# From the trunk to the up tiles: the chunks in the order first, third, second, and the up operand sums spread over the second chunk's up tiles

## The chip, the cores and the metric

The kernel runs on one core of a Trainium2 chip. The metric is the device time of one execution in microseconds (us), the median of several runs. The profile is one execution taken by the hardware profiler. Its engines: PE (TensorE, matmuls; PEld is its weight load), DVE (VectorE), ACT (ScalarE), POOL (GpSimd), and SP, which issues most DMAs. Each engine works through its own queue in order; between engines, and between DMAs and engines, semaphores order the work.

## The reference

One layer of a streaming encoder, for 1024 prompt frames and 32 sample frames of width D = 1024, 1056 columns in all:

```
h = rms_norm(x, g_mix);  z = h @ w_in -> q, k, v, conv_h, conv_B, conv_C, gate_a, gate_b
a  = window_attention(q, k, v) @ w_attn_out
bo = (conv_B * causal_conv3(conv_C * conv_h)) @ w_conv_out
x += (sigmoid(gate_a) * a + sigmoid(gate_b) * bo) @ w_mix_out
x += cross_attention(rms_norm(x, g_cross) @ w_cq, mem_k, mem_v) @ w_co     # 4 heads, 256 memory rows
x += square(relu(rms_norm(x, g_mlp) @ w_up)) @ w_down                      # hidden 4096
y  = rms_norm(x, g_final)
```

All arithmetic is float32. The sample frames have their own memory keys and values. The change touches the stages from w_conv_out to w_up.

## The kernel before

Activations lie with features on the partitions, eight blocks f of 128 features, and the 1056 columns in three chunks: chunk 0 and chunk 1 with 384 columns, chunk 2 with 288 (256 prompt and the 32 sample columns). Each float32 operand is split into a rounded high half (an ACT copy) and the remainder as low half (a DVE subtraction), and each product is three matmuls: high x high, high x low, low x high. One gemm tile is 8 x 3 = 24 matmuls into one accumulator in PSUM; there are three such accumulators (acc). Weight tiles have two raw buffers (wr) and three buffers each for high and low halves (wh, wl). issue_w splits a weight tile, two tiles ahead of its use. Every second tile of the weights that are used once per chunk is kept: its low half is stored to DRAM on first use (L162) and loaded from there later (L156) in place of the DVE subtraction.

The work is a list of items, filled in program order by item; a scheduler then decides the order within each engine, except that instructions under pin keep their program order. PE's order is fixed in the built program.

For each chunk c the trunk has 16 items: eight do_conv_out (L1030 multiplies the accumulator by the gate) and eight do_mix (L1045 adds the residual; L262 and L263 scale by the gain and split). After the trunk of a chunk come cross_steps(c): chunk_stats (the sum of squares over partitions as small matmuls pq, L214; L216 to L221 compute the inverse root; L229 and L230 put it on a diagonal; two matmuls pr, L231 and L232, spread it over the partitions; L242 copies it to R), two do_cq (queries), the units Cross (one per head, and one for the sample columns in chunk 2) with scores, turn and values, two do_co (four output features each, L1183 to L1185, added to x1 by L1187, squared by L257 and summed by POOL, L259), and chunk_stats again. These steps are laid beside the items of the next stage by beside: after each filler item comes one step. So PE has a full gemm between the short dependent steps.

The order of the chunks is 0, 1, 2. cross_steps(0) lie beside trunk(1), cross_steps(1) beside trunk(2), cross_steps(2) beside the eight up tiles of chunk 0 and the eight of chunk 1 (up0). Then follow the eight up tiles of chunk 2, and then the rest of the up product in late pairs (up_start, up_pair), which form some products by sums of operands.

The up tiles of chunks 0 and 1 take normalised operands: normed_split(c, f) multiplies by gain and R (L1212, DVE), stores the result to DRAM (xn_d), copies the high half (L1215, ACT) and subtracts (L1216, DVE); its DVE operations are pinned. For chunk 2 the operand is only scaled by the gain, and R is applied at the eviction (L1240). Chunk 0's eight normed_split stand after the fillers 6 to 13 of trunk(2), chunk 1's after the fillers 0 to 7 of up0(0) + up0(1).

combine(k), for k = 0 to 3, loads four normalised blocks from xn_d, forms the sums N3, N1, T2 and N4 (three DVE operations, one on POOL) and splits each. Before, it follows the first four up tiles of chunk 2. For k of 2 and 3, T2 and N4 are put into chunk 1's operand buffers (yslot(1)), which are free once chunk 1's up tiles are done.

Of the kernel before, what the change touches and what calls it, by code (L numbers as in the profile page):

```python
# [10 lines left out]
F32 = mybir.dt.float32  # L11
F32R = mybir.dt.float32r
AF = mybir.ActivationFunctionType
ALU = mybir.AluOpType
# [9 lines left out]
NF = 8  # L24
# [14 lines left out]
def hybrid_step(ctx: ExitStack, tc: tile.TileContext, io):  # L39
    nc = tc.nc  # L40
    act, dve, pool_e, pe, sp = nc.scalar, nc.vector, nc.gpsimd, nc.tensor, nc.sync
# [3 lines left out]
    def nm(s):  # L45
        uid[0] += 1
        return f"{s}_{uid[0]}"
# [5 lines left out]
    def closed(cm):  # L53
        cm.__exit__(None, None, None)
# [17 lines left out]
    def col(j):  # L72
        return prm[:, j : j + 1]
# [19 lines left out]
    def pin(ins):  # L93
        return tc.keep_in_program_order(ins)
# [6 lines left out]
    def tmp(n, dt=F32):  # L101
        return tp.tile([P, n], dt, tag="ct", bufs=NCT, name=nm("ct"))
# [11 lines left out]
    def item(fn, *keys):  # L114
        plan.append((fn, keys))
        worder.extend(keys)
# [127 lines left out]
    def chunk_stats(c):  # L244
        chunk_col(c)
        chunk_row(c)
# [508 lines left out]
    def yslot(c):  # L755
        return slot(Y["pool" if c < 2 else "top"], f"Y{c}", CH[c][1])
# [8 lines left out]
    def open_top():  # L765
        Y["cm"], Y["top"] = opened("ytop", bufs=16, reuse_waits="tile", side="right")
# [11 lines left out]
    def pump(n):  # L778
        for into, at, t, get in coming:
            hi, lo = into[at] = (get(), get())  # L780
            pin(act.copy(hi, t))  # L781
            pin(dve.tensor_sub(lo, t, hi.bitcast(F32)))  # L782
        coming.clear()
        for into, at, src, cols, get in wanted[:n]:
            t = cols() if callable(cols) else tmp(cols)
            sp.dma_start(t, src)
            coming.append((into, at, t, get))
        del wanted[:n]
# [76 lines left out]
    def close_gates():  # L865
        pump(0)
        assert not wanted
        closed(Y["cm"])
        open_top()
        ctx.push(Y["cm"])  # L870
        for c in (1, 2):
            wanted.extend((bcp[c], k, bc_d[c][:, k], CH[c][1], lambda c=c: yslot(c)) for k in range(NF))
        pump(2)

# [139 lines left out]
    def mslot(n):  # L1014
        return mpool.tile([P, 384], F32R, tag="M", name=nm("M"))[:, :n]
# [67 lines left out]
    def do_cq(c, j):  # L1083
        def fn(w):
            n = CH[c][1]
            a = acc_tile([P, n])
            gemm(a, w, xc[c])
            t = tmp(n)
            dve.scalar_tensor_tensor(t, a, 0.125, R[c], op0=ALU.mult, op1=ALU.mult)  # L1089
            for e in range(2):  # L1090
                own, other = slice(64 * e, 64 * e + 64), slice(64 - 64 * e, 128 - 64 * e)
                q = yslot(c)
                act.copy(q[own], t[own])
                dve.tensor_sub(q[other], t[own], q[own].bitcast(F32))
                qc[2 * j + e, c] = q

        return fn
# [109 lines left out]
    def lt(n=384):  # L1207
        return L["pool"].tile([P, n], F32, tag="lt", bufs=6, name=nm("lt"))

    def normed_split(c, f):  # L1210
        t = tmp(CH[c][1])
        pin(dve.scalar_tensor_tensor(t, x1[c][f], col(G_MLP + f), R[c], op0=ALU.mult, op1=ALU.mult))  # L1212
        sp.dma_start(xn_d[c][:, f], t)
        hi, lo = xm[c][f] = (yslot(c), yslot(c))
        act.copy(hi, t)  # L1215
        pin(dve.tensor_sub(lo, t, hi.bitcast(F32)))  # L1216
# [16 lines left out]
    def up_part(w, c, j):  # L1233
        n = CH[c][1]
        a = ps.tile([P, n], F32, tag="pt", bufs=2, name=nm("pa")) if w[0] == "late" else acc_tile([P, n])
        gemm(a, w[-2:], xm[c])
        flush()
        t = tmp(n)
        if c == 2:
            dve.scalar_tensor_tensor(t, a, 0.0, R[c], op0=ALU.max, op1=ALU.mult)  # L1240
        else:
            dve.tensor_scalar_max(t, a, 0.0)  # L1242
        h = tmp(n)
        pool_e.tensor_tensor(h, t, t, op=ALU.mult)  # L1244
        hidden(c, j, h)

    def do_up(j, c):
        return (lambda w: up_part(w, c, j)), ("w_up", j)


    comb = {}

    def comb_slot(kind, k):
        if kind in ("N1", "N3"):
            return mslot(384)
        return L["pool"].tile([P, 384], F32R, tag="hx", bufs=8, name=nm("hx")) if k < 2 else yslot(1)

    def combine(k):
        b12, b22, b11, b21 = (lt() for _ in range(4))
        for t, c, f in ((b12, 1, k), (b22, 1, k + 4), (b11, 0, k), (b21, 0, k + 4)):  # L1260
            sp.dma_start(t, xn_d[c][:, f])
        n3, n1, t2, n4 = b22, b12, b11, b21
        pin(dve.tensor_sub(n3, b12, b22))
        pin(dve.tensor_sub(n1, b11, b12))
        pin(dve.tensor_sub(t2, b11, n3))
        pin(pool_e.tensor_tensor(n4, b21, t2, op=ALU.subtract))
        for kind, x in (("T2", t2), ("N1", n1), ("N3", n3), ("N4", n4)):
            hi, lo = comb[kind, k] = (comb_slot(kind, k), comb_slot(kind, k))
            act.copy(hi, x)
            if kind[0] == "T" or kind == "N1":  # L1270
                pin(dve.tensor_sub(lo, x, hi.bitcast(F32)))
            else:
                pin(pool_e.tensor_tensor(lo, x, hi.bitcast(F32), op=ALU.subtract))

# [30 lines left out]
    def up_fetch(i):  # L1307
        if i < len(UP):
            pair_fetch(("u", i), io["w_up"][UP[i][0]], io["w_up"][UP[i][1]])

    def up_issue(i, which):
        if i < len(UP):
            pair_issue(("u", i), which)
        elif which != 2:
            if worder[wpos[0]] is STOP:
                wpos[0] += 1
            issue_w()
# [129 lines left out]
    def cross_steps(c):  # L1447
        units = [Cross(c, h) for h in ([0, 1, 2, 3] if c < 2 else [4, 0, 1, 2, 3])]
        nu = len(units)
        steps = [("call", [mem_load] if c == 0 else [mem_load_s] if c == 1 else [])]  # L1450
        steps.append(("call", [lambda: chunk_stats(c)]))
        steps.append(("items", [(do_cq(c, j), ("w_cq", j)) for j in range(2)]))
        for i in range(nu + 2):
            calls = []
            if i < nu:
                calls.append(units[i].scores)
            if 0 <= i - 2 < nu:
                calls.append(units[i - 2].values)
            if 0 <= i - 1 < nu:
                calls.append(units[i - 1].turn)  # L1460
            steps.append(("call", calls))
            if c < 2 and i < nu:
                steps.append(("call", []))
        if c == 2:
            steps.append(("call", [open_late]))
            steps.append(("call", []))
            steps.append(("call", []))
        steps.append(("items", [(do_co(c, 0), ("w_co", 0))]))
        steps.append(("items", [(do_co(c, 1), ("w_co", 1))]))
        steps.append(("call", [lambda: chunk_stats(c)]))  # L1470
        return steps

    def beside(steps, fillers, late=()):
        for i, filler in enumerate(fillers):
            item(*filler)
            for x in [x for at, x in late if at == i]:
                item(lambda x=x: x())
            if steps:
                kind, what = steps.pop(0)
                for x in what:  # L1480
                    if kind == "items":
                        item(*x)
                    else:
                        item(lambda x=x: x())
        return steps

    def trunk(c):
        return [(do_conv_out(c, f), ("w_conv_out", f)) for f in range(NF)] + [
            (do_mix(c, f), ("w_mix", f)) for f in range(NF)
        ]  # L1490

    up0 = lambda c: [do_up(j, c) for j in range(NF)]
# [2 lines left out]

    left = beside([], trunk(0), [(i, lambda: pump(2)) for i in range(NF)])
    item(lambda: pump(0))
    left = beside(cross_steps(0), trunk(1))

    normed = lambda c, at: [(at + f, lambda f=f: normed_split(c, f)) for f in range(NF)]  # L1500
    left = beside(left + cross_steps(1), trunk(2), normed(0, 6))
    left = beside(left + cross_steps(2), up0(0) + up0(1), normed(1, 0))
    assert not left
    for j in range(NF):
        item(*do_up(j, 2))
        if j < 4:
            item(lambda j=j: combine(j))
        if j == 5:
            item(lambda: [up_fetch(0), up_fetch(1), up_issue(0, 1)])
        if j == 6:  # L1510
            item(lambda: [up_issue(0, 2), up_issue(1, 1)])


# [144 lines left out]
    steps = [(j, t) for j in range(4) for t in range(2)]  # L1658
# [181 lines left out]
```

## Time and profile before

| | us |
|---|---|
| three runs | 1796.23, 1789.85, 1793.36 |
| median | 1793.36 |
| span of the profiled execution, first to last instruction | 1791.7 |
| PE busy in it | 1754.1 |
| DVE / ACT / POOL busy | 1173.1 / 799.6 / 594.2 |

The profile gives the span of its execution and no other time of it; the median of the runs is 1.7 us above the span. In its views, a row of instructions tells start, duration, engine, line, operation, out<-in with the tile names, and in brackets the idle time of the engine before and what ended it. A row of waits tells the waiting engine, tile and line, what released it, then total us, times and the longest. A row of stretches gives from:to, its length, then busy us (and instructions) of PE, PEld, DVE, ACT and POOL, PE's mean granted clock as a share of full speed, the DMA engines' busy share and GB/s. Matmuls overlap: a duration is that of one from start to end, and the distance of their starts is PE's pace.

### The profile page before, as it was taken

Reading aid. Unit: us, or ns where it says so; the run is one execution under the profiler, and the core shown is the slowest. Engines: PE = TensorE matmul, PEld = TensorE weight load, DVE = VectorE, ACT = ScalarE, POOL = GpSimd, SP = SyncE. Lnnn points to the kernel's source line nnn. Section 1 sums busy time; section 2 is a strip of 40 time slices with the busy share of each in tenths; the row PEclk is TensorE's granted clock in tenths of the full one; section 3 lists DMA queues with packets and bytes.
Section 4 is the critical chain, followed back from the end, with each engine's and each line's share of the span. In section 5 each row is a group of like instructions: output and inputs, shape, how many; then the busy total and the mean of one; then the engine's idle time right before and its main releaser. Section 6 shows DMA issues by size and latency. Waiting matters only on the chain. (4 is left out here: it accounts for less than half of the span.)

```text
span 1791.7 us, 30247 instructions
## 1 busy us (share of the span) xinstructions
PE 1754.1 (98%) x11110; PEld 1732.5 (97%) x11110; DVE 1173.1 (65%) x2165; ACT 799.6 (45%) x1566; POOL 594.2 (33%) x681
## 2 busy tenths in 40 slices
PE   8999999999999999999999989999999999999997
PEld 8999999999999999999999989999999999999997
DVE  6776767868666646546566777767566676436763
ACT  8643534435345334334565745632222343324453
POOL 0013146553453444511224142386554300100111
PEclk9999999999999999999999999999999999999999
DMA  5232234344346888758765657754333487446673
GB/s 181 98 116 92 87 104 153 118 142 144 137 151 239 286 281 282 270 196 274 261 208 201 229 187 252 254 180 148 131 127 137 150 291 246 144 131 214 198 234 125
DMA packets 183858, 331.50 MB, mean 185 GB/s; under 512 B 18768, under 2 KB 139376, under 8 KB 183584
## 3 DMA queue, kind: packets, MB, share of 16 engines
q1 hardware_dynamic: 169936, 281.18, 46.7%
q0 software_dynamic: 13776, 48.41, 7.6%
q8 instruction: 87, 1.43, 0.3%
q14 instruction: 59, 0.48, 0.1%
HBM read 242.99 MB, written 86.52 MB: 184 GB/s over the span
## 5 line engine op out<-in xcount | busy, mean ns | idle before, releaser
L126 DVE TENSOR_TENSOR wl<-wr,wh 128x1024 fp32r<-128x1024 f32 x225 | 300.9, 1337 | 178.6 <-ACT wh L125 175.8
L125 ACT CAST wh<-wr 128x1024 fp32r<-128x1024 f32 x225 | 236.8, 1052 | 401.1 <-PE acc L1587 103.1
L183 PE MATMUL acc<-X,wh 128*128 128x384 f32 (+1 forms) x864 | 282.2, 327 | 8.2 <-ACT wh L125 8.2
L184 PE MATMUL acc<-X,wh 128*128 128x384 f32 (+1 forms) x864 | 279.4, 323 | 0.0
L185 PE MATMUL acc<-X,wl 128*128 128x384 f32 (+1 forms) x864 | 278.9, 323 | 0.3 <-DVE wl L126 0.3
L183 PE MATMUL acc<-Y,wh 128*128 128x384 f32 (+1 forms) x624 | 201.9, 325 | 0.8 <-DVE ct L1242 0.3
L185 PE MATMUL acc<-Y,wl 128*128 128x384 f32 (+1 forms) x624 | 202.1, 324 | 0.0
L184 PE MATMUL acc<-Y,wh 128*128 128x384 f32 (+1 forms) x624 | 201.7, 324 | 0.0
L259 POOL TENSOR_TENSOR xacc<-xacc,ct 128x384 f32<-128x384 f32 (+1 forms) x62 | 75.4, 1218 | 339.8 <-ACT ct L257 334.2
L183 PEld LDWEIGHTS acc<-X,wh 128*128 128x128 f32 x864 | 163.2, 189 | 8.8 <-ACT wh L125 8.2
L184 PEld LDWEIGHTS acc<-X,wh 128*128 128x128 f32 x864 | 163.5, 189 | 0.6
L185 PEld LDWEIGHTS acc<-X,wl 128*128 128x128 f32 x864 | 163.1, 189 | 0.8 <-DVE wl L126 0.8
L183 PEld LDWEIGHTS acc<-Y,wh 128*128 128x128 f32 x624 | 117.4, 189 | 1.8 <-DVE ct L1089 0.6
L185 PEld LDWEIGHTS acc<-Y,wl 128*128 128x128 f32 x624 | 117.8, 189 | 0.0
L184 PEld LDWEIGHTS acc<-Y,wh 128*128 128x128 f32 x624 | 117.7, 189 | 0.0
L1586 PE MATMUL acc<-Y,wh 128*128 128x384 f32 (+1 forms) x352 | 112.7, 322 | 1.1 <-DVE lt L1378 0.7
L1587 PE MATMUL acc<-Y,wh 128*128 128x384 f32 (+1 forms) x352 | 113.1, 321 | 0.0
L1588 PE MATMUL acc<-Y,wl 128*128 128x384 f32 (+1 forms) x352 | 112.8, 321 | 0.0
L125 ACT CAST PTh<-pt 128x512 fp32r<-128x512 f32 (+3 forms) x94 | 46.2, 517 | 115.8 <-PE pt L572 107.8
L707 POOL TENSOR_TENSOR xacc<-xacc 128x256 f32<-128x256 f32 x92 | 83.7, 909 | 4.9
L851 PE MATMUL acc<-Y,wh 128*128 128x384 f32 x248 | 83.1, 336 | 1.8 <-ACT wh L125 1.8
L1244 POOL TENSOR_TENSOR ct<-ct 128x288 f32<-128x288 f32 (+1 forms) x48 | 45.2, 943 | 116.7 <-DVE ct L1240 45.7
(360 smaller groups left out, 4759.5 us busy)
## 6 DMA issues: line engine op xcount, KB each, us to landing
wr<-in_w_in SPq DMA_DIRECT2D x53, 512.0 KB, 3.5
wr<-in_w_up SPq DMA_DIRECT2D x48, 512.0 KB, 4.0
wr<-in_w_down SPq DMA_DIRECT2D x32, 512.0 KB, 4.0
wr<-wsum_d SPq DMA_DIRECT2D x32, 512.0 KB, 3.9
wl<-wl_d SPq DMA_DIRECT2D x28, 512.0 KB, 4.6
wr<-in_w_conv_out SPq DMA_DIRECT2D x24, 512.0 KB, 4.4
wr<-in_w_mix SPq DMA_DIRECT2D x24, 512.0 KB, 4.4
ct<-b_d SPq DMA_DIRECT2D x48, 192.0 KB, 4.1
```

The costliest lines, as they stand in the source:

```text
L125: act.copy(hi, src)
L126: dve.tensor_sub(lo, src, hi.bitcast(F32))
L183: pe.matmul(out, wh[:, a], hi, start=(k == 0), stop=False)
L184: pe.matmul(out, wh[:, a], lo, start=False, stop=False)
L185: pe.matmul(out, wl[:, a], hi, start=False, stop=(k == len(acts) - 1))
L259: pool_e.tensor_tensor(acc, acc, sq, op=ALU.add)
L707: pin(pool_e.tensor_tensor(t[:, to], t[:, x], t[:, y], op=ALU.add))
L851: pe.matmul(acc, wh[:, a], hi, start=(start and k == 0), stop=False, skip_group_check=True)
L1244: pool_e.tensor_tensor(h, t, t, op=ALU.mult)
L1586: pe.matmul(a, wh[:, s], hi, start=(start and k == 0), stop=False, skip_group_check=True)
L1587: pe.matmul(a, wh[:, s], lo, start=False, stop=False, skip_group_check=True)
L1588: pe.matmul(a, wl[:, s], hi, start=False, stop=(stop and k == len(acts) - 1), skip_group_check=True)
```

## The change

The chunks go in the order 0, 2, 1. cross_steps(0) lie beside trunk(2), cross_steps(2) beside trunk(1), and cross_steps(1) beside the eight up tiles of chunk 0 and the first five of chunk 2. Chunk 0's normed_split follow the odd fillers 1 to 15 of trunk(1). Chunk 1's eight normed_split stand together after those 13 up tiles, then come chunk 1's eight up tiles, and the last three of chunk 2. cross_steps(2) no longer have two empty steps before do_co, and those of chunk 1 have no empty step after each unit. The sample's memory values are loaded at the end of the units of chunk 0.

combine(k) now follows chunk 1's up tiles 1, 3, 5 and 7. For k of 2 and 3 it only splits N1 and N3; T2 and N4 are split by combine_rest after the chunk 2 tiles 5 and 6. The first late weights are fetched one tile later, counted from the end.

```diff
-        for c in (1, 2):
+        for c in (2, 1):
             wanted.extend((bcp[c], k, bc_d[c][:, k], CH[c][1], lambda c=c: yslot(c)) for k in range(NF))
...
+    held = {}
+
     def combine(k):
...
-        for kind, x in (("T2", t2), ("N1", n1), ("N3", n3), ("N4", n4)):
-            hi, lo = comb[kind, k] = (comb_slot(kind, k), comb_slot(kind, k))
-            act.copy(hi, x)
-            if kind[0] == "T" or kind == "N1":
-                pin(dve.tensor_sub(lo, x, hi.bitcast(F32)))
-            else:
-                pin(pool_e.tensor_tensor(lo, x, hi.bitcast(F32), op=ALU.subtract))
+        comb_split("N1", k, n1)
+        comb_split("N3", k, n3)
+        held[k] = t2, n4
+        if k < 2:
+            combine_rest(k)
+
+    def combine_rest(k):
+        for kind, x in zip(("T2", "N4"), held.pop(k)):
+            comb_split(kind, k, x)
+
+    def comb_split(kind, k, x):
+        hi, lo = comb[kind, k] = (comb_slot(kind, k), comb_slot(kind, k))
+        act.copy(hi, x)
+        if kind in ("T2", "N1"):
+            pin(dve.tensor_sub(lo, x, hi.bitcast(F32)))
+        else:
+            pin(pool_e.tensor_tensor(lo, x, hi.bitcast(F32), op=ALU.subtract))
...
     def cross_steps(c):
         units = [Cross(c, h) for h in ([0, 1, 2, 3] if c < 2 else [4, 0, 1, 2, 3])]
         nu = len(units)
-        steps = [("call", [mem_load] if c == 0 else [mem_load_s] if c == 1 else [])]
+        last = c == 1
+        steps = [("call", [mem_load] if c == 0 else [])]
...
-            if c < 2 and i < nu:
+            if c == 0 and i < nu:
                 steps.append(("call", []))
-        if c == 2:
+        if c == 0:
+            steps[-1][1].append(mem_load_s)
+        if last:
             steps.append(("call", [open_late]))
-            steps.append(("call", []))
-            steps.append(("call", []))
...
-    left = beside(cross_steps(0), trunk(1))
-
-    normed = lambda c, at: [(at + f, lambda f=f: normed_split(c, f)) for f in range(NF)]
-    left = beside(left + cross_steps(1), trunk(2), normed(0, 6))
-    left = beside(left + cross_steps(2), up0(0) + up0(1), normed(1, 0))
+    left = beside(cross_steps(0), trunk(2))
+
+    normed = lambda c, ats: [(at, lambda f=f: normed_split(c, f)) for f, at in enumerate(ats)]
+    left = beside(left + cross_steps(2), trunk(1), normed(0, range(1, 16, 2)))
+    left = beside(left + cross_steps(1), up0(0) + up0(2)[:5])
     assert not left
+    for f in range(NF):
+        item(lambda f=f: normed_split(1, f))
     for j in range(NF):
+        item(*do_up(j, 1))
+        if j in (1, 3, 5, 7):
+            item(lambda k=j // 2: combine(k))
+    for j in range(5, NF):
         item(*do_up(j, 2))
-        if j < 4:
-            item(lambda j=j: combine(j))
-        if j == 5:
+        if j < 7:
+            item(lambda k=j - 3: combine_rest(k))
+        if j == 6:
             item(lambda: [up_fetch(0), up_fetch(1), up_issue(0, 1)])
-        if j == 6:
+        if j == 7:
             item(lambda: [up_issue(0, 2), up_issue(1, 1)])
```

## The prediction

> **What bounds the kernel now.** I read the page's busy times first, then a table of stretches, then PE's waits.
>
> ```profile
> span 1791.7 us, 30247 instructions
> ...
> PE 1754.1 (98%) x11110; PEld 1732.5 (97%) x11110; DVE 1173.1 (65%) x2165; ACT 799.6 (45%) x1566; POOL 594.2 (33%) x681
> ```
>
> PE is busy for all but 37.6 us of the span. The change adds and removes no matmul (the same tiles with the same weights in another order), so it can only take away or add PE idle time, and time at a reduced clock. The rows of a stretch table show where both lie around the change (second number: PE's busy time; the number behind POOL's: granted clock):
>
> ```profile
> 948.00:966.00 18.00, 16.96 (x93) 15.43 (x92) 10.13 (x17) 9.61 (x16) 10.86 (x10) 1.00 0.56 194
> 1026.00:1056.00 30.00, 23.36 (x128) 20.82 (x128) 24.31 (x39) 16.06 (x29) 14.18 (x16) 0.89 0.57 192
> 1132.00:1150.00 18.00, 16.82 (x105) 15.91 (x104) 12.32 (x24) 11.98 (x26) 6.92 (x7) 1.00 0.90 322
> 1172.00:1184.00 12.00, 10.20 (x63) 9.96 (x62) 10.04 (x11) 5.17 (x8) 11.15 (x9) 0.86 0.88 300
> 684.00:694.00 10.00, 7.09 (x25) 6.51 (x24) 4.30 (x7) 3.68 (x6) 4.05 (x6) 0.66 0.76 274
> ```
>
> The first three are the output projections of cross attention (do_co) of chunks 0, 1 and 2: PE idles 1.04, 6.64 and 1.18 us. The fourth is the start of the late up tiles (1.80 us); the fifth lies ahead of the change and is used for the clock. Chunk 1 stands out, and PE's waits in 1026:1056 begin so:
>
> ```profile
> PE acc L1183 <- DVE Gb L1045: 3.4, 3, 1.5
> PE o L1156 <- DVE tO L1159: 1.3, 1, 1.3
> PE acc L1183 <- DVE Ga L1187: 0.9, 1, 0.9
> ```
>
> They end on DVE, which is busy 24.31 of these 30 us: chunk 0's eight normed_split and the short 288-column mix tiles fall on the same stretch. Its clock of 0.89 takes 0.11 x 30 = 3.3 us, of which 23.36/30, 2.6 us, fell on busy time. The pile-up is worth 6.6 + 2.6 = 9.2 us, and it is nearly all that the change can win.
>
> **Part 1: the pile-up of chunk 1 goes (-9.2, then +1.2).** Its do_co now stands beside up tiles of chunk 2, whose eviction is one DVE and one POOL operation, and chunk 0's normed_split are spread over every other item of trunk(1). Late next are the projection's own evictions, as for chunks 0 and 2: 1.04 and 1.18 us above. I take 1.2.
>
> **Part 2: do_co of chunk 0 (+0.5).** It moves from mix tiles of chunk 1 to the shorter ones of chunk 2. It cost 1.04 us with the long ones; with the short ones and normed_split on top, 9.2. Without normed_split it is nearer to the first: I take 1.5, and keep 9.2 as the upper end.
>
> **Part 3: do_co of chunk 2 (+3.9).** It loses the two empty steps before it: its five units had nine up tiles beside them until do_co, now seven tiles of the trunk. In the built program's order the last head's scores stand behind mix(1,2), and no full tile follows until do_co's first half is over, since that half claims all three accumulators. The last head's chain is then exposed. Its pieces, from the timeline of before:
>
> ```profile
> 1119.15 0.69 DVE L1123 TENSOR_REDUCE nmx<-sc 128x2 f32<-128x512 f32 x1 [0.56 <-PE sc L1120]
> ...
> 1121.20 0.62 DVE L1128 TENSOR_SCALAR S<-S,rec 128x256 f32<-128x256 f32 x2
> ...
> 1130.45 0.28 PE L1156 MATMUL o<-PTh,mv 128*128 128x256 f32 x1
> ...
> 1131.10 0.37 ACT L1158 COPY tO<-o 64x256 f32<-64x256 f32 x1 [1.14 <-PE o L1156]
> 1131.25 0.60 PE L1137 MATMUL pt<-ident,S 128*128 128x128 f32 x4
> ...
> 1132.07 0.76 DVE L126 TENSOR_TENSOR PTl<-pt,PTh 128x256 fp32r<-128x256 f32 x2
> ...
> 1132.74 0.41 DVE L1167 TENSOR_TENSOR Y<-tO,Y 64x256 fp32r<-64x256 f32 x1
> ```
>
> Softmax 2.67 us (1119.15 to 1121.82), transposes with split 1.58 (1131.25 to 1132.83), values 0.65, output split 2.05 (1131.10 to 1133.15): 6.95 us. PE's pace I take from twelve 384-column matmuls of do_co:
>
> ```profile
> 958.49 0.33 PE L1183 MATMUL acc<-Y,wh 128*128 128x384 f32 x1
> ...
> 960.39 0.34 PE L1185 MATMUL acc<-Y,wl 128*128 128x384 f32 x1
> ```
>
> 1.90/11 = 0.173 us each, by columns 0.130 for 288 and 0.115 for 256. Beside the chain PE has 12 value matmuls (1.4), 8 transposes (about 0.9) and 9 projection matmuls (1.2): 3.5 us. So 3.4 us stay idle, against 1.2 before. Such a gap has a second price:
>
> ```profile
> PE acc L851 <- ACT wh L125: 2.9, 1, 2.9
> ```
>
> After this one wait (at 684 us) the clock of 684:694 was 0.66, 3.4 us lost; after the 1.80 us of 1172:1184 it was 0.86, 0.14 x 12 = 1.7 us. I add 1.7: 3.4 + 1.7 - 1.2 = 3.9. [...] Bounds: 0, if the units run ahead as they did before, to 10, if trunk(1)'s evictions and normed_split stand in DVE's queue between the links.
>
> **Part 4: chunk 1's statistics are now the last thing before its own up tiles (+9.3).** Before, eight up tiles of chunk 0 and eight of chunk 1 stood between, and chunk 2 needed its statistics only at eviction. Now PE's order reads: do_co's second half, one up tile of chunk 2 (24 x 0.130 = 3.1 us), the statistics, then three up tiles of chunk 1 interleaved feature by feature. They can't start before the first normed_split:
>
> ```profile
> 1062.46 0.72 PE L214 MATMUL pq<-ones,xacc 128*128 128x1 f32 x6
> ```
> ```profile
> 1155.07 0.15 DVE L216 TENSOR_SCALAR st_v<-pq 128x3 f32<-128x3 f32 x1
> ...
> 1156.80 0.81 DVE L230 SCALAR_TENSOR_TENSOR ct<-ident,rc,ct 128x128 fp32r<-128x128 f32 x3 [0.55 <-ACT ct L229]
> ```
> ```profile
> 1070.89 0.48 ACT L242 COPY R<-pr 128x384 f32<-128x384 f32 x1 [3.51 <-PE pr L232]
> ```
> ```profile
> L1212 DVE SCALAR_TENSOR_TENSOR ct<-Gb,prm,R x10: 602/610/1387, 1026.2 to 1101.8; 128x384 f32<-128x384 f32 x10
> ```
> ```profile
> L1215 ACT CAST Y<-ct x16: 508/515/523, 1007.9 to 1103.9; 128x384 fp32r<-128x384 f32 x16
> ```
> ```profile
> L1216 DVE TENSOR_TENSOR Y<-ct,Y x16: 540/554/1029, 1010.1 to 1105.5; 128x384 fp32r<-128x384 f32 x16
> ```
> ```profile
> L126 DVE TENSOR_TENSOR wl<-wr,wh x225: 1208/1226/2308, 8.1 to 1767.9; 128x1024 fp32r<-128x1024 f32 x113
> ```
> ```profile
> L125 ACT CAST wh<-wr 128x1024 fp32r<-128x1024 f32 x225 | 236.8, 1052 | 401.1 <-PE acc L1587 103.1
> ```
>
> From st_v to the end of the three L230: 2.54; two matmuls that spread the row, 0.6; copy of R, 0.48; normed_split's first two, 0.61 + 0.52; four hand-overs, 0.2: 5.0 us. Ahead of st_v in DVE's queue stands the split of the third up weight, which waits for its cast, and that for the last tile to free a weight buffer: 0.2 + 1.05 + 1.23 = 2.5 us behind that tile. PE works about 1.1 us of these 7.5, 0.7 of it for the sums over partitions (L214's row above): 6.4 idle. (POOL's sums end about 1 us behind the tile, covered by the weight; if they came 2 us later, add 1.) Then normed_split is pinned in order, each waiting for its ACT cast: 0.61 + 0.52 + 0.55 + 0.15 = 1.83 us a feature against PE's 9 x 0.173 = 1.56; eight of them with the tail cost 1.9. The clock is low behind such a gap, but DVE sets the pace there: I count 1.0 of the 3.4 us. Sum 9.3; bounds 5 (the split done early, full clock) and 14 (weight late, clock low throughout).
>
> **Part 5: the weights behind the interleaved tiles (+5.2).** The three tiles hold all three weight buffers to their end. The fourth tile's low half, a reload from DRAM (up(3,1) is one of the kept ones), can be issued only then; before it in SP's queue stand chunk 1's eight normed stores and six loads for combine, some of which wait for a store to land, but the last of them can go about as early.
>
> ```profile
> DMA to landing us min/median/max: 3.3/4.6/6.6
> ```
>
> For this reload (L156) 4.6 us. Release and issue add about 0.3, and PE has eight matmuls left for that time, 1.4 us: 3.5 idle, and 1.7 of clock. Bounds 2.2 and 9.
>
> **Parts at nothing.** The combine operations are the same, half of them later: N4 and T2 of two k are needed only at the first late pair, after the late start's own tiles; if late, the price is a wait as in 1172:1184. That start keeps its 1.8 + 1.7.
>
> **Sum.** -9.2 + 1.2 + 0.5 + 3.9 + 9.3 + 5.2 = +10.9 us. On the profiled span, 1791.7, that is 1802.6; the page gives no other time of that execution. The median of the runs, 1793.36, is 1.7 above the span, so the forecast is 1804.
>
> **The rivals.** (a) Faster: the swap mainly removes the pile-up, and the drain overlaps. It decides from the point where parts 3 to 5 together stay under 9.2 - 1.7 = 7.5 us, less what else goes. At their lower ends, 0 - 1.2 + 5 + 2.2, they cost 6.0, so -1.5; with the late start's 3.5 gone too (its weights fetched with DVE free of combine), -5.0 and under: 1788. For it: DVE's load is clearly better spread; against it: PE's order is fixed, and nothing fills the drain. (b) A draw: the drain near its lower end, or the reload early, about 1794 to 1798. (c) Slower by more: the pile-up only moves, to do_co of chunk 0 beside the short mix tiles (9.2 in place of 1.5) or to the drain at its upper end: +15 to +24, about 1812. For it: the short tiles; against it: normed_split isn't there any more.
>
> **How the numbers follow.** A difference of 0.3%, 5.4 us, is about what a measurement tells from no change: faster is under 1788, slower over 1798.8. Forecast (1799 to 1809) 0.47, (c) 0.20, (b) 0.21, (a) 0.12. So slower 0.67, same 0.21, faster 0.12. The range from 1791 to 1816 leaves out most of (a) and the end of (c).
>
> **What would show it.** Right: no stretch like 1026:1056 beside mix tiles; one gap of 6 to 7 us on PE behind the tile up(4,2), ended by the ACT cast L1215; L1215 and L1216 as releasers eight times; then a gap of 3 to 4 us ended by a DMA of wl; a gap of about 3 us in chunk 2's do_co, each with a low clock behind it. Wrong: PE busy through chunk 1's statistics, a reload that is there in time, or the old DVE waits at L1183 beside chunk 2's mix tiles.

## The result, and the profile after

| | before | after |
|---|---|---|
| median of five runs, us | 1793.36 (1789.85 to 1796.23) | 1803.07 (1798.39 to 1804.87) |
| ratio after / before, 95% interval | | 1.0052 (1.0034 to 1.0070) |
| profiled execution, us (span) | (1791.7) | 1799.48 (1797.6) |

The change makes the kernel 9.3 us slower, 6.1 to 12.6 by the interval. The forecast was 1804.0. The page of the kernel after:

```profile
span 1797.6 us, 30252 instructions
...
PE 1757.5 (98%) x11110; PEld 1737.5 (97%) x11110; DVE 1165.8 (65%) x2165; ACT 797.8 (44%) x1566; POOL 589.3 (33%) x681
```

The same 11110 matmuls. The two spans lie only 5.9 us apart, and that must not be read as the price: the wait at 684 us, far ahead of the change (2.9 us, and a clock of 0.66 over 684:694, in the profile of before), is 0.3 us at a clock of 1.00 in this one, and it varies between profiles of kernels that are alike up to there. So stretches are compared, and totals by the runs. The table of stretches of after (columns as before; the second number is PE's busy time, the one behind POOL's the granted clock):

```profile
820.00:860.00 40.00, 37.01 (x190) 35.71 (x189) 26.13 (x42) 19.70 (x36) 6.56 (x6) 0.91 0.72 241
925.00:955.00 30.00, 27.58 (x174) 26.63 (x174) 18.02 (x28) 16.92 (x27) 16.27 (x17) 0.94 0.60 203
1010.00:1042.00 32.00, 26.75 (x150) 25.25 (x149) 25.03 (x49) 21.39 (x51) 12.94 (x12) 0.89 0.44 147
1110.00:1130.00 20.00, 19.32 (x125) 18.01 (x123) 13.60 (x21) 10.93 (x18) 9.27 (x9) 1.00 0.72 258
1130.00:1162.00 32.00, 24.33 (x122) 22.54 (x121) 18.15 (x35) 12.73 (x22) 7.90 (x9) 0.84 0.64 208
1184.00:1210.00 26.00, 26.00 (x178) 26.00 (x177) 14.98 (x15) 9.35 (x15) 23.27 (x19) 1.00 0.40 138
```

From the second row on these are do_co of chunk 0, of chunk 2 and of chunk 1, chunk 1's statistics with the three interleaved tiles, and the late start. Chunk 1's pile-up is gone: 0.68 us idle at full clock. The late start's stall is gone too. In their place stand 5.25 us idle at chunk 2's do_co and 7.67 at the statistics, both with a low clock (0.89 and 0.84), and 2.42 at chunk 0's do_co. PE's waits in the statistics' stretch (1130:1162) begin:

```profile
PE pr L231 <- ACT ct L229: 3.4, 1, 3.4
PE acc L183 <- ACT Y L1215: 1.8, 1, 1.8
PE acc L185 <- DMA wl<-wl_d: 1.1, 1, 1.1
PE pq L214 <- POOL xacc L259: 0.8, 1, 0.8
```

The first, second and fourth are the drain, 6.0 us, one chain in three pieces, as its timeline shows:

```profile
1133.67 0.83 PE L214 MATMUL pq<-ones,xacc 128*128 128x1 f32 x6 [0.80 <-POOL xacc L259]
1134.42 1.23 DVE L126 TENSOR_TENSOR wl<-wr,wh 128x1024 fp32r<-128x1024 f32 x1 [0.99 <-ACT wh L125]
1135.56 0.15 DVE L216 TENSOR_SCALAR st_v<-pq 128x3 f32<-128x3 f32 x1
1137.35 0.88 DVE L230 SCALAR_TENSOR_TENSOR ct<-ident,rc,ct 128x128 fp32r<-128x128 f32 x3 [0.60 <-ACT ct L229]
1137.87 0.69 PE L231 MATMUL pr<-ct,ones_r 128*128 128x384 f32 x1 [3.37 <-ACT ct L229]
1139.57 0.62 DVE L1212 SCALAR_TENSOR_TENSOR ct<-Ga,prm,R 128x384 f32<-128x384 f32 x1 [1.35 <-issue]
1140.78 1.33 PE L183 MATMUL acc<-Y,wh 128*128 128x384 f32 x3 [1.82 <-ACT Y L1215]
```

The third weight's split (1134.42) stands in DVE's queue ahead of st_v, which so starts 1.1 us after the sums over partitions are done (1134.50).

### The profile page after: what moved, and what is told of

It reads as the page before. It is cut to its first block, busy times and chain, and to the rows that moved or that the text cites. A ratio compares the mean times of both kernels' runs of the same rounds, so it can differ in the third digit from the quotient of the medians.

```text
span 1797.6 us, 30252 instructions
## 1 busy us (share of the span) xinstructions
PE 1757.5 (98%) x11110; PEld 1737.5 (97%) x11110; DVE 1165.8 (65%) x2165; ACT 797.8 (44%) x1566; POOL 589.3 (33%) x681
## 4 chain that ended last, share of the span: by engine, by line
PE 85%; DMA 7%; DVE 3%; ACT 2%; issue 1%; POOL 1%; SPq 0%; DVEq 0%; ACTq 0%; POOLq 0%
PE acc L183 13%; PE acc L185 13%; PE acc L184 13%; PE acc L1606 6%; PE acc L1605 6%; PE acc L1607 6%; PE acc L851 5%; PE acc L852 5%; PE acc L853 5%; PE pa L184 2%; PE pa L183 2%; PE pa L185 2%; PE pt L572 2%; DMA wr<-in_w_conv_out 1%; DVE wl L126 1%
## 5 line engine op out<-in xcount | busy, mean ns | idle before, releaser
L126 DVE TENSOR_TENSOR wl<-wr,wh 128x1024 fp32r<-128x1024 f32 x225 | 297.2, 1321 | 177.2 <-ACT wh L125 175.2
L707 POOL TENSOR_TENSOR ws<-ws 128x256 f32<-128x256 f32 x92 | 82.3, 895 | 5.2
L853 PE MATMUL acc<-Y,wl 128*128 128x384 f32 x248 | 83.3, 336 | 0.0
```

What stands on the lines that cost most here:

```text
L126: dve.tensor_sub(lo, src, hi.bitcast(F32))
L707: pin(pool_e.tensor_tensor(t[:, to], t[:, x], t[:, y], op=ALU.add))
L853: pe.matmul(acc, wl[:, a], hi, start=False, stop=(k == 3), skip_group_check=True)
```

## The experiments

For each kernel the table gives the ratio to the kernel before, from runs on the same chip, and an excess by stage, worked out from the trace: the distances between the starts of successive matmuls, less PE's steady pace for their sizes, summed. It holds idle time and reduced clock alike; stages are of one profiled execution, and some us of a difference can be that execution's: e1_gap's took 1805.99 us with a median of 1802.01, e2_fill's 1797.58 with 1802.63. "Trunk 0" is chunk 0's trunk; "cross" runs from the first statistics to the first up eviction, "up" from there to the late start, "late" through the late pairs.

| kernel | ratio (95%) | trunk 0 | cross | up | late |
|---|---|---|---|---|---|
| before | 1 | 3.4 | 13.3 | 6.2 | 3.7 |
| after | 1.0052 (1.0034 to 1.0070) | 7.1 | 17.2 | 14.3 | 0.5 |
| e1_gap | 1.0050 (1.0036 to 1.0063) | 7.7 | 12.2 | 19.7 | 0.6 |
| e2_fill | 1.0049 (1.0035 to 1.0063) | 6.6 | 12.9 | 11.6 | 1.6 |
| e4_both | 1.0040 (1.0026 to 1.0055) | 6.7 | 13.6 | 13.4 | 1.7 |
| e5_fill3 | 1.0063 (1.0045 to 1.0081) | 7.4 | 13.3 | 13.1 | 1.6 |
| e6_nokeep3 | 1.0075 (1.0055 to 1.0095) | 7.4 | 14.6 | 19.1 | 0.7 |
| e8_all | 1.0019 (1.0008 to 1.0030) | 7.1 | 10.9 | 10.2 | 3.4 |
| e11_all4 | 1.0022 (1.0012 to 1.0032) | 8.9 | 10.7 | 10.1 | 3.9 |
| e12_tile_behind | 1.0027 (1.0013 to 1.0041) | 6.3 | 11.3 | 10.7 | 3.6 |
| e9_co0 | 1.0078 (1.0061 to 1.0095) | 5.6 | 19.4 | 16.1 | 0.5 |
| e3_before_early | 1.0001 (0.9990 to 1.0012) | 3.1 | 14.1 | 6.2 | 3.3 |
| e10_before_co1 | 1.0037 (1.0025 to 1.0050) | 4.1 | 11.1 | 10.5 | 9.4 |
| e7_before_rest | 1.0001 (0.9989 to 1.0013) | 3.3 | 13.1 | 5.5 | 6.6 |

**The last head of chunk 2.** After, with the two empty steps back:

```diff
         if last:
             steps.append(("call", [open_late]))
+        if c == 2:
+            steps.append(("call", []))
+            steps.append(("call", []))
```

> The changed kernel with the two empty steps put back before do_co of chunk 2. Theory (part 3): the last head's chain was exposed because no full tile followed it; with two more trunk tiles beside it, PE's idle time around that do_co falls from 5.2 us to about 1.5 and the low clock behind it goes: 5 us less than the changed kernel, about 1798. Rival: the chain is late because trunk(1) with its normed_split loads DVE and ACT; then the idle time stays at 4 us or more and the time within 2 us of the changed kernel's 1803.

The cross stage lost the 5 us, and the stretch shows where:

```profile
1010.00:1042.00 32.00, 29.62 (x180) 28.66 (x180) 26.29 (x55) 22.84 (x58) 14.20 (x12) 0.95 0.53 169
```

2.38 us idle in place of 5.25. But the up stage rose by 5.4, with a wait for an up tile's eviction (L1240) that is 0.3 us in after, and a longer one for the reload:

```profile
PE pr L231 <- ACT ct L229: 3.7, 1, 3.7
PE acc L185 <- DMA wl<-wl_d: 3.2, 1, 3.2
PE acc L1183 <- DVE ct L1240: 2.2, 1, 2.2
```

So the step's price in its place is confirmed, and the whole kernel gains nothing that the runs show. How much of the 5.4 us the edit brings on stays open, since the profiled execution lies 4 us above the median.

**Tiles into the drain.** After, with the up tiles 5 and 6 of chunk 2 moved ahead of chunk 1's normed_split (e2_fill; tile 7 stays at the end), the same with the two empty steps (e4_both), and with all three tiles (e5_fill3, shown). The fetch of the late weights stays one tile ahead of the end, and combine_rest stands at the end:

```diff
     assert not left
+    for j in (5, 6, 7):
+        item(*do_up(j, 2))
     for f in range(NF):
         item(lambda f=f: normed_split(1, f))
```

> The changed kernel with two more up tiles of chunk 2 (5 and 6) between the last do_co of chunk 1 and its normed_split; one is left for the end. Theory (part 4): the drain of 7 us is hidden but for the last links behind the spread row (about 2 us), and the clock stays up: 5 to 8 us less than the changed kernel, about 1796, unless the late start, with one tile ahead of it in place of three, waits for its weights (then up to 4 us of that is given back). Rival: the cost of the drain is mostly the pinned DVE pace of normed_split and the low clock; then no more than 2 us are won.

> Both edits together. Theory: their savings add, 10 to 13 us less than the changed kernel, about 1791, at or a little under the kernel before, since the pile-up of 9 us is gone and the exposed chains nearly so. Rival: they share the clock or a DVE queue and give no more than the larger of the two, about 1796.

> All three remaining up tiles of chunk 2 stand before chunk 1's normed_split, so PE's order has the sums over partitions (pq) inside the first of them and the spreading matmuls (pr) inside the last, one matmul before its end. Theory (the drain is a chain of 5.0 us from st_v to the first operand with nothing on PE beside it): only the part behind pr is still exposed, copy of R, the first scaling and the cast, 0.5 + 0.6 + 0.5 plus hand-overs, 1.8 to 2.3 us in one gap instead of the 7.0 us of three; the excess of the up stage, 14.3 us in the kernel after, goes to 6 to 9, and the time 4 to 7 us below the kernel after (ratio to before 1.000 to 1.003) unless the end pays for it. Rival 1: the tiles are missed where they stood: the late start has no tile of its own ahead any more, its weights come late, and the stage of late pairs gives back 2 to 5 us (ratio 1.003 to 1.006). Rival 2: the time lost in the up stage is not the drain's but that of three interleaved tiles and their weights: ratio 1.004 to 1.006, the excess moves by under 3 us.

The wait for pr goes in all three, and PE's longest wait becomes L1215's, 3.2, 3.2 and 3.5 us, with 2.3 to 2.7 us for the reload: the drain is halved, and the ratios hardly move: 1.0040, the lowest, still overlaps the interval of after, so the two savings of e4_both don't add as its theory had it. Why a gap stays shows the timeline of e5_fill3:

```profile
1142.56 0.34 PE L232 MATMUL pr<-ct,ones_r 128*128 128x384 f32 x1
1142.80 1.04 ACT L125 CAST wh<-wr 128x1024 fp32r<-128x1024 f32 x1 [2.31 <-PE acc L184]
...
1143.87 0.48 ACT L242 COPY R<-pr 128x384 f32<-128x384 f32 x1
1143.88 1.54 DVE L126 TENSOR_TENSOR wl<-wr,wh 128x1024 fp32r<-128x1024 f32 x1 [0.29 <-ACT wh L125]
1145.34 0.60 DVE L1212 SCALAR_TENSOR_TENSOR ct<-Ga,prm,R 128x384 f32<-128x384 f32 x1
```

L232 stands one matmul before the end of the last tile, and the next weight's cast on ACT and split on DVE come ahead of the copy of R and the first scaling. The "1.8 to 2.3 us" expected became 3.5; the theory that a chain with nothing beside it is the whole price fell, the rival on weights (excess moved by under 3 us, here 1.2) fits better.

**The reload.** After, with up(3,1)'s low half made by DVE each time:

```diff
+    kept.pop(("w_up", 3))
```

> The kernel after, but the fourth up weight (up(3, all chunks)) is not kept: its low half is made by the DVE subtraction every time, and not stored and loaded. Theory (part 5: the reload of that low half, issued when the three interleaved tiles free a buffer, is what PE waits for behind them): PE's wait for a DMA of wl goes (1.1 us in the profile of the kernel after, 2.5 to 3.4 in three variants of it), its place is taken by a wait for the DVE split of at most 1 us, since the raw weight was loaded before; total 1 to 3 us less than the kernel after, ratio to before 1.0035 to 1.0045. Rival: the buffer is what comes late, not the reload: cast and subtraction (1.05 + 1.2 us) stand behind it just as long, a wait of 2 to 3 us for the DVE split appears, and the time stays, ratio 1.0045 to 1.0055.

```profile
PE acc L1183 <- DVE ct L1240: 2.5, 1, 2.5
...
PE acc L185 <- DVE wl L126: 1.3, 1, 1.3
```

The wait only changes its name, from 1.1 us for the DMA to 1.3 for DVE; the buffer is what comes late, as the rival said. It came out slower than foreseen by both: the eviction wait of e1_gap is here too. There a weight's split stands ahead of that eviction in DVE's queue, and the split's cast on ACT waits 3.5 us for the raw load, against 1.0 in after. The loads of raw weights in the 20 us around the wait, first in this kernel, then in after (the slowest matters here):

```profile
DMA to landing us min/median/max: 3.1/4.4/8.6
```
```profile
DMA to landing us min/median/max: 3.1/5.0/7.2
```

Whether the edit does that isn't settled: e1_gap has the wait without the edit, with a load of up to 8.5 us there too, and e8_all with the edit has 0.4 us of it.

**All three together, and one tile more.** e8_all joins the three edits. e11_all4 leaves out chunk 1's empty first step as well, so that four tiles stand behind the statistics; e12_tile_behind puts the last of these four behind normed_split:

```diff
-        steps = [("call", [mem_load] if c == 0 else [])]
+        steps = [("call", [mem_load] if c == 0 else [])] if c != 1 else []
...
-    for j in (5, 6, 7):
+    for j in (5, 6):
         item(*do_up(j, 2))
     for f in range(NF):
         item(lambda f=f: normed_split(1, f))
+    item(*do_up(7, 2))
```

> Three edits on the kernel after together: all three remaining up tiles of chunk 2 before chunk 1's normed_split, the two empty steps before chunk 2's do_co back, the fourth up weight not kept. Theory (the loss of the change is the sum of the exposed last head of chunk 2, the drain and the reload): 5 + 5 + 1 us come back of the 9.4 lost, while the pile-up of chunk 1 and the late start's stall stay away, so ratio to before 0.997 to 1.001. Rival: each filled gap only lets the next step run up against its own weights or evictions, and about half comes back: ratio 1.002 to 1.004.

> The kernel with the three edits together (three up tiles in the drain, two empty steps, no kept fourth weight), and the first, empty step of chunk 1's cross steps left out, so that four up tiles of chunk 2 stand behind chunk 1's statistics and not three. Theory (what is left of the drain, 3.7 us idle and 1.7 of clock, is there because the second of the two spreading matmuls stands at the very end of the last tile, and the next weight's cast and subtraction are ahead of the copy of R and the first scaling): with one tile more the first operand is there when the tile ends, and 3 to 5 us go: ratio 0.9985 to 1.001. Rival: the matmuls move with the tiles and the weight's split stays ahead of the scaling: the gap stays over 2 us, ratio 1.001 to 1.003.

> The kernel with the four edits, and chunk 1's normed_split moved ahead of chunk 2's last up tile in program order: three tiles behind chunk 1's statistics, then normed_split, then the fourth tile. In the built order the first scaling stands ahead of that tile's eviction on DVE and not behind it. Theory (what is left of the drain, 1.8 + 0.9 us in the kernel with four edits, is the first scaling, which waits in DVE's queue behind the eviction of the last tile, though R is there 4 us before): no gap over 0.6 us between chunk 2's last up tile and chunk 1's first ones, the excess of the up stage goes from 10.1 to 6 to 8 us, near the 6.2 of the kernel before, ratio 0.9995 to 1.0012. Rival: the splits of the weights on DVE between the normed_split set the pace of the three interleaved tiles, and the loss returns in them or behind them as a wait for a weight: excess 9 to 11, ratio 1.0015 to 1.003.

e8_all has a ratio of 1.0019, clearly under after's 1.0052: about two thirds of the loss come back by these edits, 3.4 us stay. That lies between the two ranges, a little below the rival's. The next two win nothing further. In e11_all4 R is there at 1140.2 and the first scaling starts at 1144.17, behind the last tile's eviction:

```profile
1139.70 0.48 ACT L242 COPY R<-pr 128x384 f32<-128x384 f32 x1 [1.63 <-PE pr L232]
...
1143.80 0.46 DVE L1240 SCALAR_TENSOR_TENSOR ct<-acc,R 128x288 f32<-128x288 f32 x1 [2.64 <-PE acc L185]
1144.17 0.61 DVE L1212 SCALAR_TENSOR_TENSOR ct<-Ga,prm,R 128x384 f32<-128x384 f32 x1
```

In e12_tile_behind the scaling is early and PE has no wait for L1215 left. Its waits of 1105:1170 begin otherwise:

```profile
PE acc L185 <- DMA wl<-wl_d: 1.9, 1, 1.9
PE acc L185 <- DVE wl L126: 1.2, 1, 1.2
```

The first wait ends at 1144 us, in the interleaved tiles of chunk 1: it stands at a matmul of 384 columns, so one of them, and not the moved tile with its 288, now waits for its low half, reloaded from DRAM. The rival was right: the loss returns as waits for weights, 1.0027. No kernel of the new order beats the kernel before.

**The pile-up.** The prediction put it down to DVE's load, normed_split and short mix tiles together. Before, with chunk 0's normed_split six fillers earlier:

```diff
-    left = beside(left + cross_steps(1), trunk(2), normed(0, 6))
+    left = beside(left + cross_steps(1), trunk(2), normed(0, 0))
```

> The kernel before with chunk 0's eight normed_split behind the fillers 0 to 7 of trunk(2) in place of 6 to 13; nothing else is changed. Theory (what part 1 removes): the pile-up at chunk 1's do_co is the meeting of normed_split with short mix tiles; without it PE's idle time in the 30 us around that do_co falls from 6.6 to about 2 us and the clock stays up: 6 to 8 us less than before, about 1786. Rival: the short tiles alone make it; then the idle time stays over 4 us and the time within 3 us of before.

```profile
1026.00:1056.00 30.00, 26.04 (x163) 24.44 (x162) 18.64 (x31) 16.62 (x28) 16.54 (x16) 0.94 0.60 202
```

DVE's busy time in the stretch falls from 24.31 to 18.64 us, 3.96 us stay idle, the rest moves ahead of the stretch (cross 14.1 against 13.3), and the ratio is 1.0001. So normed_split isn't needed for most of the loss in this place. It isn't free where it went either: from 1005 to 1026 us PE idles 3.1 us with DVE busy 18.1 of the 21, where before it idles not at all with 17.2. So the run doesn't clear DVE's load as a part of the cause. After, with chunk 0's do_co on trunk(1)'s conv_out tiles:

```diff
+        if c == 0:
+            steps.extend(("call", []) for _ in range(3))
         steps.append(("items", [(do_co(c, 0), ("w_co", 0))]))
...
-    left = beside(left + cross_steps(2), trunk(1), normed(0, range(1, 16, 2)))
+    left = beside(left + cross_steps(2), trunk(1), normed(0, (3, 5, 7, 9, 11, 13, 14, 15)))
```

> The kernel after with three empty steps before chunk 0's do_co: it moves from chunk 2's mix tiles (288 columns) to the first conv_out tiles of trunk(1) (384 columns, no residual and no split behind them); chunk 0's normed_split follow the fillers 3, 5, 7, 9, 11, 13, 14, 15, and the steps of chunk 2 stand three fillers later. Theory (the loss at an output projection comes from the short mix tiles beside it, whose evictions and splits on DVE and ACT hold back the projection's own): chunk 0's do_co costs 1 to 1.5 us and not the 4.6 of the kernel after; the stretch from the first statistics to the first up eviction loses 3 us of its excess of 17.2, unless chunk 2's do_co, now beside later mix tiles and normed_split, takes it; ratio 1.003 to 1.0045. Rival: an output projection costs 3 to 5 us wherever it stands without its empty steps, because its three accumulators are claimed at once: the excess stays at 16 to 18, ratio 1.0045 to 1.006.

```profile
930.00:960.00 30.00, 29.21 (x187) 28.89 (x187) 19.76 (x30) 16.50 (x26) 17.39 (x17) 1.00 0.68 242
1018.00:1058.00 40.00, 30.99 (x164) 29.71 (x164) 31.99 (x63) 24.04 (x60) 14.84 (x14) 0.83 0.39 136
```

Chunk 0's do_co falls to 0.79 us idle at full clock, as the theory had it. But the edit does two things at once, it takes the mix tiles away and puts three more tiles between the last head and do_co. Of PE's 2.4 us in after, 1.0 is a wait for a mix eviction (L1045) and 0.8 one for the last head (L1165), and this run doesn't part the two. And chunk 2's units, now three fillers later beside mix tiles and normed_split, idle 9.0 us at a clock of 0.83, more than is won, so that the ratio, 1.0078, is above both ranges. And before, with chunk 1's do_co on chunk 0's up tiles (chunk 2 loses its first empty step and the two before its do_co for it):

```diff
+        if c == 1:
+            steps.extend(("call", []) for _ in range(3))
...
-    left = beside(left + cross_steps(2), up0(0) + up0(1), normed(1, 0))
+    left = beside(left + cross_steps(2), up0(0) + up0(1), normed(1, (3, 3, 4, 4, 5, 5, 6, 6)))
```

> The kernel before, order of the chunks unchanged, but chunk 1's do_co and second statistics stand three steps later, so that they lie beside the first up tiles of chunk 0 and not beside chunk 2's mix tiles; chunk 1's normed_split follow in pairs after the fillers 3 to 6, and chunk 2 loses its first empty step and the two before its do_co. Theory (the pile-up of 6.6 us idle and 2.6 of clock in the kernel before is made by the short mix tiles beside do_co): it falls to 2 to 4 us; chunk 2's last head, beside up tiles, costs at most 2 us more; 3 to 6 us less than before, ratio 0.9965 to 0.9985, the fastest of all kernels here. Rival 1: normed_split of chunk 1, now in pairs, or chunk 2's exposed chain takes it back: ratio 0.999 to 1.002. Rival 2: with the mix tiles alone the stretch at 1026 to 1056 us keeps its gaps, as it kept them when normed_split was moved out of it: 1.000 to 1.002.

```profile
1020.00:1050.00 30.00, 24.47 (x143) 21.97 (x142) 23.73 (x37) 15.08 (x27) 11.04 (x12) 0.94 0.68 238
1125.00:1147.00 22.00, 17.44 (x107) 15.46 (x107) 16.76 (x32) 16.00 (x37) 8.50 (x9) 1.00 0.68 240
```

With the mix tiles and last units of chunk 1 still there, 5.5 us stay in the old place, and chunk 2's last head and do_co idle 4.6. Both rivals hold in part; 1.0037 is above what any of the three gave. Three of the troubled stretches have one thing in common in DVE's own waits, first before (1026:1056), then e3_before_early (the same), then after at chunk 0's do_co (925:955):

```profile
DVE Gb L1045 <- DMA ct<-in_x: 2.4, 2, 2.0
```
```profile
DVE Gb L1045 <- DMA ct<-in_x: 6.1, 3, 4.5
```
```profile
DVE Gb L1045 <- DMA ct<-in_x: 4.8, 3, 3.5
```

The mix tile's eviction waits for the residual input, loaded from DRAM, at the head of DVE's queue, and the projection's evictions wait behind it. It can only be a part of the cause. In before, 1.5 of the 3.4 us that PE waited for Gb (L1045) came without it: that eviction, at 1034.19, followed a normed_split scaling and others on a busy DVE, and 1.9 us came behind a late input. In e9_co0 the quiet stretch has such waits of 3.9 us (925:955), and the worst one, 1018:1058, has none from 1020 to 1052 us. No run with earlier input loads was made, so the pile-up's cause stays open between late inputs, DVE's load and the last head's chain.

**The late start.** Before, with T2 and N4 of k = 2 and 3 split after the up tiles 4 and 5 of chunk 2 (the change's second part alone):

```diff
     for j in range(NF):
         item(*do_up(j, 2))
...
+        if j in (4, 5):
+            item(lambda k=j - 2: combine_rest(k))
```

> The kernel before with the change's second part alone: for k of 2 and 3, T2 and N4 are split after the fifth and sixth up tiles of chunk 2 and not with the other sums. The order of the chunks is untouched. Theory (the late start's stall in the kernel before, 1.8 us of idle time and 1.7 of clock at 1172 to 1184 us, comes from the four sums pressed into the first four tiles, and the spreading removes it): the stretch of the late start loses 2 to 3.5 us, ratio to before 0.998 to 0.999. Rival: the stall comes from the late weights, not the sums, and in the kernel after it went because their fetch stands elsewhere: the stall stays as it was, ratio 0.9995 to 1.0005.

The ratio is 1.0001. PE still idles there, 4.67 us in 1165:1210 at full clock, against 2.13 at a clock of 0.96 before, but most of it has other releasers. Before, a weight's cast had the longest wait, 1.8 us; here it has 0.9, and PE's waits in 1160:1215 begin:

```profile
PE acc L851 <- ACT xacc L1353: 1.7, 1, 1.7
PE acc L851 <- ACT s L1347: 1.2, 1, 1.2
```

Those are the copies and the relu of the late pairs on ACT, for which PE waits to get its accumulators back. The rival's ratio fits, but the stall isn't as it was, and the spreading alone neither helps nor harms. What frees the late start in after was not isolated; it isn't the three tiles of chunk 2 ahead of it, since e5_fill3, without them, has no wait there either (late excess 1.6 us, none of it at the start).

## Why the prediction was right

The sum was right, several of its terms were not, and that they nearly cancel is luck: of the six parts below four are off by 2.5 to 3.5 us, two up and two down. With each term taken as the prediction did, idle time plus lost clock on busy time:

| part | forecast | in the trace |
|---|---|---|
| 1, chunk 1's pile-up | -9.2 + 1.2 = -8.0 | -9.2 + 0.7 = -8.5 |
| 2, chunk 0's do_co | +0.5 | 2.4 + 0.06 x 27.58 - 1.0 = +3.0 |
| 3, chunk 2's do_co | +3.9 | 5.25 + 0.11 x 26.75 - 1.2 = +7.0 |
| 4, drain | 6.4 + 2.9 = +9.3 | 6.0 + 2.8 = +8.8 |
| 5, reload | +5.2 | 1.1 + 0.6 = +1.7 |
| at nothing, late start | 0 | -1.8 - 1.7 = -3.5 |
| sum | +10.9 | +8.5 |

(In part 4, the 72 matmuls of the interleaved tiles take 15.3 us, 1140.7 to 1156.0, against 72 x 0.173 = 12.5. In part 5, 0.6 are two waits for casts.) The runs give +9.3.

**Part 1 was right in its place** and size; its reason was at best a part of it (the pile-up, above). **Part 2 failed** at "without normed_split it is nearer to the first": chunk 0's do_co lost 3.0 us more with no normed_split beside it, and e3_before_early keeps 3.96 us idle without it. Whether the mix tiles or the last head's chain makes up the loss, e9_co0 leaves open. That is rival (c), and it was partly true: 3.0 us, not the upper end.

**Part 3: the mechanism was right, the size was off**, and its upper bound's reason is in the trace, "trunk(1)'s evictions ... in DVE's queue between the links":

```profile
1016.50 0.56 DVE L1045 TENSOR_TENSOR Ga<-acc,ct 128x384 f32<-128x384 f32 x1 [0.82 <-DMA ct<-in_x]
1016.97 0.68 DVE L1123 TENSOR_REDUCE nmx<-sc 128x2 f32<-128x512 f32 x1
...
1018.68 0.40 DVE L1159 TENSOR_TENSOR tO<-o,tO 64x256 f32<-64x256 f32 x1
1019.14 0.38 PE L1156 MATMUL o<-PTh,mv 128*128 128x256 f32 x1 [2.90 <-DVE tO L1159]
```

The eviction of mix(1,2) waits 0.82 us for its input, and the last head's softmax and the previous head's output add stand behind it. The clock's price was right as a kind: half speed from 1020.3 and from 1027.1 us for 3.41 us each, behind gaps of 2.9 and 1.3; the clock over the stretch (1010:1042) is 0.89.

**Part 4 was right to half a microsecond**, with one swap inside. The 1.9 us of DVE pace and 1.0 of clock came out as clock alone: behind the drain PE ran at half speed from 1136.4 for 10.24 us, one matmul in 0.32 us and so nine of a feature in 2.9, slower than DVE, whose features follow each other in 1.66 us (L1212 at 1139.57 and 1146.24, four apart), not 1.83. So L1215 was named once as releaser, not eight times. And the gap came in three pieces, since the sums over partitions, held back by POOL, and the two spreading matmuls lie in it.

**Part 5 was over-sized**: 1.1 us of wait for the reload and no low clock. In e1_gap, e2_fill and e5_fill3 the same wait is 3.2, 2.3 and 2.7 us, so 3.5 was near a spread of which after shows the low end. **"That start keeps its 1.8 + 1.7" was wrong**: the stall went, and the two errors nearly cancel those of parts 2 and 3.

**One loss was not in the prediction at all.** Chunk 0's own trunk costs 5.6 to 8.9 us of excess in the ten kernels of the new order and 3.1 to 4.1 in the four of the old one, 3.6 us more on average. Before, the stretch reads

```profile
820.00:860.00 40.00, 37.62 (x211) 36.17 (x210) 28.76 (x47) 22.46 (x41) 7.79 (x7) 1.00 0.79 267
```

against a clock of 0.91 after. Nine of the ten have a half-clock period that begins between 836 and 852 us, none of the four has one. In after most of it is clock: two such periods, from 836.0 and 849.6, cost about 1.7 us each (half of 3.41, an estimate). What of the change reaches there is the order in which the other two chunks' inputs are loaded and split beside this trunk, chunk 2's 288 columns now first and chunk 1's 384 behind, and with it the built order at the turn from conv_out to mix. One wait there can be followed. ACT's rows, before and then after:

```profile
848.43 1.05 ACT L125 CAST wh<-wr 128x1024 fp32r<-128x1024 f32 x1
851.09 0.41 ACT L1068 CAST mv<-mvr 128x256 fp32r<-128x256 f32 x1 [1.61 <-DMA mvr<-in_cmem_v]
851.40 1.04 ACT L125 CAST wh<-wr 128x1024 fp32r<-128x1024 f32 x1
```
```profile
846.19 0.40 ACT L1068 CAST mv<-mvr 128x256 fp32r<-128x256 f32 x1 [2.56 <-DMA mvr<-in_cmem_v]
846.50 1.99 ACT L125 CAST wh<-wr 128x1024 fp32r<-128x1024 f32 x2
```

Before, one mix weight is cast ahead of the last memory-value cast (L1068), which waits for its load; after, two weights stand behind it. PE's longest wait for a weight's cast there is 1.7 us in all four kernels of the old order and 2.4 to 3.1 in eight of the new ones (1.2 in after, 0.3 in e1_gap). So a late memory load (an idle ACT for 1.61 us before, 2.56 after) holds back weights on ACT; that this is what makes the clock fall is not shown, and no part was tried alone. With this loss the terms come to +12.1, at the upper end of the interval. The two profiles fit that: 5.9 us apart, and about 6 us more with the wait at 684 us and its clock set aside.

## What to carry to other kernels

Count, for a stage that is to lose its neighbour, not one gap but the whole row of things queued for the same moment: statistics, first operand, weight split, buffer release. Here a filled gap uncovered a next wait of 1 to 3 us, and three edits together brought back two thirds where the single ones brought nothing that the runs could show. Look at what the engine that is waited for waits for itself: a DVE that seemed overloaded stood, for part of the time, behind a late input load (2.4 us in 1026:1056 before). And a right total may rest on errors that cancel: the terms have to be checked one by one.

## What was unexpected of the hardware

- In the traces of before and after the clock runs at half speed for 3.41, 6.83 or 10.24 us at a time, steps of 3.41 (the last period of each, 8.2 and 8.0 us, reaches past the end of the span), and the length of a gap didn't tell whether it fell. In the kernel after it fell at 836.0 us behind waits of 0.7 and 0.8 us, and again at 849.6 behind 1.2 and 0.3 (0.91 over 820 to 860); in e10_before_co1 it was 1.00 over a stretch with 4.6 us idle in 22 (above), and in e11_all4 through a gap of 1.6 us with another of 0.7 behind it:

```profile
1138.00:1150.00 12.00, 9.64 (x64) 8.81 (x63) 6.79 (x10) 4.17 (x7) 2.03 (x3) 1.00 0.84 275
```

- A half-clock period can outweigh the engine that seemed to set the pace: behind the drain PE at half speed took 2.9 us for a feature, DVE 1.66 for its operands.
- The load of one weight tile took 3.1 to 8.6 us from issue to landing within 20 us of one kernel (e6_nokeep3), and the same wait in unchanged code came out at 2.9 and 0.3 us in two profiles. A difference of a few us between two single profiles can't be put down to an edit without the stretch that shows it.
